# A first stage in a hand-written order: squares on two engines, sums on TensorE tile by tile, held-back loads and filler matmuls

## The chip, the cores and the metric

The kernel runs on one NeuronCore of a Trainium2 chip. The core has five engines that work side by side and meet only through semaphores: TensorE (PE in the profile, with its weight loads shown apart as PEld), VectorE (DVE), ScalarE (ACT), GpSimd (POOL) and SyncE (SP, which here only issues DMAs). [...] The metric is the device time of one launch in microseconds. Before the change three runs took 1020.61, 1021.97 and 1024.64 us, so the median is 1021.97 us.

## The reference

One inference step of a small diffusion backbone of two layers, on 128 context tokens and 256 latent tokens (384 columns in all), with 1024 features. Everything is fp32. What the first stage of the kernel computes is the start of layer 0:

```
def rmsnorm(x, g):
    xf = x.astype(jnp.float32)
    y = xf * lax.rsqrt(jnp.mean(xf * xf, axis=-1, keepdims=True) + EPS)
    return (y * g.astype(jnp.float32)).astype(x.dtype)

def adaln(cond, w_ada, b_ada):
    mod = jax.nn.silu(cond) @ w_ada + b_ada
    return jnp.split(mod[:, None, :], 6, axis=-1)

def modulate(h, shift, scale):
    return h * (1 + scale) + shift
...
    for l in range(DEPTH):
        sm, cm, gm, sf, cf, gf = adaln(c, w_ada[l], b_ada[l])
        h = modulate(rmsnorm(x, norm_mix_g[l]), sm, cm)
        j = l // N_MIXERS
        if l % N_MIXERS == 0:
            q, k, v = qkv_proj(h, w_qkv[j])
            o = neighbourhood_attention(q, k, v, cache_k[:, j], cache_v[:, j], rpb[j])
            mix = merge_heads(o) @ w_attn_out[j]
        else:
            mix = chunk_gmlp(h, w_gmlp_in[j], g_gmlp_v[j], w_spatial[j], b_spatial[j], w_gmlp_out[j])
        x = x + gm * mix
        h = modulate(rmsnorm(x, norm_ffn_g[l]), sf, cf)
        x = x + gf * conv_ffn(h, w_ffn_up[l], w_ffn_conv[l], b_ffn_conv[l], w_ffn_down[l])
```

The context tokens take the same path with a conditioning vector of their own and plain attention. The change is in the part from the load of `x` to the end of `h @ w_v`, the value projection of layer 0.

## The kernel before

The activations lie transposed: feature tile `x[k]` (k = 0 to 7) is 128 features on the partitions by 384 tokens. `GROUPS` splits the tokens into columns 0 to 127 (context) and 128 to 383 (latent), since the two have different modulation vectors.

A product that must keep fp32 accuracy is made of three matmuls (`mac`, L101): each operand is split into a rounded part `hi` and a rest `lo`, and hi*hi, hi*lo and lo*hi are summed in PSUM. For a weight tile, `load` (L88) issues a 512 KB DMA into a staging tile `st` (three buffers), ACT casts it to `hi` (L96), and DVE subtracts to get `lo` (L97). For the activations, `modulated` (L323) makes `u = x * scale * R` on DVE (L326), `hhi = u + shift` on ACT (L328) and `hlo` on DVE (L330), each once per token group.

The first stage runs as follows. SP issues the eight loads of `x` (L66), then the weights of the first modulation block `adw` (L127, two DMAs of 512 KB each), the tables `b_ada` (L132) and `prm` (L134), and then for each k one value-weight tile `st` and the next modulation block. ACT squares the tiles of `x`, DVE adds seven of them up in `sqacc` (L271), and six matmuls with a column of ones (`sums`, L282, for the total of seven and for the last tile) sum over the features. `rsqrt` (L306 to L316) turns the sums into `r` on DVE and POOL, and three matmuls with the identity (L300) spread `r` over all partitions as `R`, which ACT copies to SBUF (L409). A modulation block (`ada_block`, L136) is 16 small matmuls (L145) of the conditioning vectors with `adw`, a copy to SBUF on ACT (L149), a transpose on TensorE (L151) and three short DVE operations (L154, L157, L117) that write the shift and scale columns `mod` of one feature tile. Then for each k come the modulated tile, the value-weight tile, modulation block k + 1, and 18 matmuls (6 products of a 128-token block with a 512-column half) into six PSUM banks `acc` that stay open for all eight k. At the end ACT copies the six banks to `V`.

At the very start 18 matmuls of a tile of ones (`warm`, L80) run on TensorE while nothing else is there for it. fp32 matmuls show as two records each in the trace, a pass each.

The tile framework's scheduler sets the order of this stage on each engine, by priorities; only the matmuls that are marked `keep_in_program_order` are fixed. The attention loop behind it has its order written out by hand (`tc.manual_schedule`, L578): there each engine runs its instructions in the order of the program. In both cases an engine runs strictly in its order, so a waiting instruction holds up all behind it on that engine.

## Time and profile before

| what | value |
|---|---|
| runs before, median of three | 1021.97 us |
| profiled execution, its time | 1021.36 us |
| its span, first to last instruction | 1019.6 us |
| share of the chain that ended last: PE | 91% |
| first value matmul starts | 17.89 us |
| last value matmul is issued, and the next products start | 63.81 us |
| mean granted TensorE clock over the span | 0.993 |

All times in views of the trace count from the span's first instruction. The span leaves out 1.8 us of the profiled execution's own time. TensorE is busy nearly from end to end (98% of the span), so the stage's part of the total is when its last value matmul is done: what comes behind it follows on without a change of order.

### The profile page before, as it was taken

The numbers are of one execution on the slowest core, as the hardware profiler recorded it, in microseconds if no ns is written. First come the engines' busy times: TensorE is split into PE (matmuls) and PEld (weight loads), VectorE is DVE, ScalarE is ACT, GpSimd is POOL, SyncE is SP. The second block draws the span as 40 slices with busy tenths as digits, with TensorE's granted clock in tenths as the row PEclk, the third lists the DMA queues.
The fourth block names the chain that finished last, engine by engine and source line by source line (L and its number), as shares of the span: only waits on it lengthen the run. The fifth ranks groups of instructions, "written<-read, shape, count | busy, mean of one in ns | idle before, by whom it ended". The sixth has DMA issues, their size and how long they took to land.

```text
span 1019.6 us, 15979 instructions
## 1 busy us (share of the span) xinstructions
PE 998.2 (98%) x6030; PEld 948.6 (93%) x6030; DVE 775.7 (76%) x1588; ACT 480.6 (47%) x841; POOL 14.7 (1%) x29
## 2 busy tenths in 40 slices
PE   7999999999999999999999999999999999999996
PEld 6788888789999999999998889999999999999996
DVE  3546566577999888999979989888598777777652
ACT  3355556557655555433354434343485444443331
POOL 1000000000000000000000000000000000000000
PEclk8999999999999999999999999999999999999999
DMA  7874645633465545576737746566325434335521
GB/s 277 310 233 143 214 172 201 227 103 126 136 191 169 163 147 161 146 240 205 225 119 257 241 158 200 179 207 186 104 83 166 144 124 125 124 114 171 161 72 62
DMA packets 53932, 172.96 MB, mean 170 GB/s; under 512 B 6224, under 2 KB 12512, under 8 KB 53856
## 3 DMA queue, kind: packets, MB, share of 16 engines
q1 hardware_dynamic: 52992, 170.11, 51.9%
q0 software_dynamic: 432, 1.06, 0.3%
q8 instruction: 47, 0.77, 0.3%
q10 hardware_dynamic: 432, 0.79, 0.2%
q14 instruction: 29, 0.24, 0.1%
HBM read 169.31 MB, written 2.62 MB: 169 GB/s over the span
## 4 chain that ended last, share of the span: by engine, by line
PE 91%; DMA 3%; ACT 2%; DVE 1%; issue 1%; SPq 1%; POOL 0%; POOLq 0%; ACTq 0%
PE bank L103 28%; PE bank L105 28%; PE bank L104 28%; DMA kT<-in_ckT 2%; DMA adw<-in_w_ada 1%; PE bank L781 1%; PE bank L145 1%; PE bank L566 1%; PE bank L517 1%; PE bank L190 1%; PE bank L549 1%; PE bank L282 0%; ACT pr L534 0%; SPq L66 0%; PE bank L300 0%
## 5 line engine op out<-in xcount | busy, mean ns | idle before, releaser
L96 ACT CAST hi<-st 128x1024 fp32r<-128x1024 f32 (+1 forms) x192 | 197.7, 1031 | 302.3 <-PE bank L104 249.0
L105 PE MATMUL bank<-hhi,lo 128*128 128x384 f32 (+1 forms) x960 | 325.1, 339 | 0.2 <-DVE lo L109 0.2
L103 PE MATMUL bank<-hhi,hi 128*128 128x384 f32 (+1 forms) x960 | 325.0, 339 | 0.0
L104 PE MATMUL bank<-hlo,hi 128*128 128x384 f32 (+1 forms) x960 | 324.7, 338 | 0.0
L97 DVE TENSOR_TENSOR lo<-st,hi 128x1024 fp32r<-128x1024 f32 (+1 forms) x192 | 229.9, 1198 | 67.9 <-ACT hi L96 67.6
L105 PEld LDWEIGHTS bank<-hhi,lo 128*128 128x128 f32 x960 | 181.1, 189 | 0.5 <-DVE lo L109 0.5
L103 PEld LDWEIGHTS bank<-hhi,hi 128*128 128x128 f32 x960 | 181.1, 189 | 0.4 <-ACT kT L473 0.2
L104 PEld LDWEIGHTS bank<-hlo,hi 128*128 128x128 f32 x960 | 180.4, 188 | 0.1
L248 DVE CUSTOM_DVE_ANT_0 junk<-adw,cs 128x1024 bf16<-128x1024 f32 x112 | 136.5, 1219 | 1.0
L105 PE MATMUL bank<-ahi,lo 128*128 128x384 f32 x352 | 118.9, 338 | 0.0
L104 PE MATMUL bank<-alo,hi 128*128 128x384 f32 x352 | 118.9, 338 | 0.0
L103 PE MATMUL bank<-ahi,hi 128*128 128x384 f32 x352 | 118.7, 338 | 0.0
L104 PEld LDWEIGHTS bank<-alo,hi 128*128 128x128 f32 x352 | 66.1, 188 | 0.0
L105 PEld LDWEIGHTS bank<-ahi,lo 128*128 128x128 f32 x352 | 66.1, 188 | 0.0
L103 PEld LDWEIGHTS bank<-ahi,hi 128*128 128x128 f32 x352 | 66.1, 188 | 0.0
L103 PE MATMUL bank<-hi,hhi 128*128 128x512 f32 x144 | 57.6, 404 | 1.8 <-ACT hhi L328 1.8
L104 PE MATMUL bank<-lo,hhi 128*128 128x512 f32 x144 | 57.4, 398 | 0.0
L105 PE MATMUL bank<-hi,hlo 128*128 128x512 f32 x144 | 57.3, 399 | 0.0
L374 DVE SCALAR_TENSOR_TENSOR x<-bank,mod,x 128x128 f32<-128x128 f32 x64 | 23.8, 412 | 35.9 <-PE bank L105 35.9
L103 PE MATMUL bank<-mhi,hi 128*128 128x384 f32 x128 | 43.3, 339 | 0.0
L105 PE MATMUL bank<-mhi,lo 128*128 128x384 f32 x128 | 43.2, 338 | 0.0
L104 PE MATMUL bank<-mlo,hi 128*128 128x384 f32 x128 | 43.1, 337 | 0.0
(154 smaller groups left out, 1268.4 us busy)
## 6 DMA issues: line engine op xcount, KB each, us to landing
st<-in_w_up SPq DMA_DIRECT2D x88, 512.0 KB, 3.6
adw<-in_w_adaT SPq DMA_DIRECT2D x56, 512.0 KB, 3.7
adw<-in_w_ada SPq DMA_DIRECT2D x40, 512.0 KB, 5.8
st<-in_w_down SPq DMA_DIRECT2D x32, 512.0 KB, 3.6
st<-in_w_qk SPq DMA_DIRECT2D x16, 512.0 KB, 3.6
st<-in_w_gu SPq DMA_DIRECT2D x16, 512.0 KB, 4.3
st<-in_w_gv SPq DMA_DIRECT2D x16, 512.0 KB, 4.5
st<-in_w_gout SPq DMA_DIRECT2D x16, 512.0 KB, 4.4
```

Source lines behind the costliest of these rows:

```text
L96: nc.scalar.copy(hi[:, :n], st[:, :n])
L97: nc.vector.tensor_tensor(lo[:, :n], st[:, :n], hi[:, :n].bitcast(F32), ALU.subtract)
L103: nc.tensor.matmul(out, a[0], b[0], start=start, stop=False)
L104: nc.tensor.matmul(out, a[0], b[1], start=False, stop=False)
L105: nc.tensor.matmul(out, a[1], b[0], start=False, stop=stop)
L145: nc.tensor.matmul(pa[32 * j:32 * j + 32, 0:P], cond_s[:, 4 * hf + kk, :], w[hf][:, kk, P * q:P * q + P], start=(kk == 0), stop=(kk == 3), ...
L190: nc.tensor.matmul(self.pa[32 * j:32 * j + 32, 0:256], cond_s[:, k, :], t[:, 256 * j:256 * j + 256], start=(k == 0), stop=(k == KD - 1), t ...
L248: tc.keep_in_program_order(nc.vector.tensor_tensor_reduce(self.junk, t, self.cs[c], 1.0, 0.0, ALU.mult, ALU.add, m[:, c:c + 1]))
L374: nc.vector.scalar_tensor_tensor(x[m][:, a:b], ps[:, a:b], mod(l, gate, m, c), x[m][:, a:b], ALU.mult, ALU.add)
L517: nc.tensor.matmul(sc[hh][:, cols], q[qp][HS[hh], qs:qs + P], k[kp][HS[hh], ks], start=i == 0, stop=i == 2)
L549: nc.tensor.transpose((ta[:, o:o + P] if g < 2 else tb[:, o - 512:o - 512 + P]), pr[:, b, g * P:g * P + P], ident)
L566: nc.tensor.matmul(pv[64 * hh:64 * hh + 64, cols], vv[:, P * t + 64 * hh:P * t + 64 * hh + 64], pT[hh][:, o:o + n], start=start, stop=stop ...
```

## The change

The first stage, too, is put under `manual_schedule`, for PE, ACT, DVE and SP, and is written out anew:

- Loads of `x` alternate between the SP queue and the ACT queue; `b_ada` and `prm` go through POOL's queue, behind `cond`, and no longer through SP's.
- The 18 warm-up matmuls are replaced by `busy(n)`: n matmuls of a bf16 tile of ones, 128x512, into a bank that is not yet in use. They stand at ten places of TensorE's order, 26 in all: 8 at the start, 1 behind the sums of each of the tiles 0 to 5, 2 ahead of the first modulation block's matmuls, 2 ahead of its transpose, and 8 ahead of the first value matmul.
- ACT squares the even tiles, DVE the odd ones. There is no `sqacc`: TensorE sums every tile by itself (3 matmuls for each, 24 in all).
- The first two value-weight loads wait, through a small DVE memset into their staging tile (`v_load(True)`), until DVE is through with its squares and with `r`; the modulation blocks are loaded two ahead.
- For k = 0 the modulated tile reads `R` straight from PSUM; the copy of `R` to SBUF comes behind it on ACT, and the `lo` part of the first weight tile is made in two halves around `hlo`.
- For each k the order is: one product (3 matmuls), the 16 matmuls of modulation block k + 1, one product, the transpose of block k + 1, four products. The DVE order in a step is `mod`, `u`, `hlo`, `lo`.
- The last tile's products are split, three and three, with the copies to `V` shared between ACT and DVE and the first q/k weight tile made ready between them.

From the first q/k product on, the order on every engine is what it was.

```
+    written = tc.manual_schedule(engines={mybir.EngineType.PE, mybir.EngineType.Activation,
+                                          mybir.EngineType.DVE, mybir.EngineType.SP})
+    written.__enter__()
+    x = [cst.tile([P, NT], F32, name=f"x{k}") for k in range(KD)]
+    for k in range(KD):
+        (nc.sync, nc.scalar)[k % 2].dma_start(x[k], xT_in[:, k, :])
     cond = cst.tile([P, KD, 2], F32, name="cond")
     nc.gpsimd.dma_start(cond, cond_in)
-    x = [cst.tile([P, NT], F32, name=f"x{k}") for k in range(KD)]
-    for k in range(KD):
-        nc.sync.dma_start(x[k], xT_in[:, k, :])
+    b_ada = cst.tile([P, 2, 48], F32, name="b_ada")
+    nc.gpsimd.dma_start(b_ada, b_ada_in)
+    prm = cst.tile([P, NPRM], F32, name="prm")
+    nc.gpsimd.dma_start(prm, prm_in)
...
-    warm = bank(ps_ad)
-    for _ in range(18):
-        nc.tensor.matmul(warm[:, :P], ones, ones, start=True, stop=True)
...
+        def busy(n):
+            for _ in range(n):
+                nc.tensor.matmul(acc[4], fill[:, 0:P], fill, start=True, stop=True)
+
+        def v_load(late):
+            st = stg.tile([P, 1024], F32, name="st", tag="st")
+            if late:
+                nc.vector.memset(st[:, 0:1], 0.0)
+            return st
...
+        def shaped(k, R, between=None):
+            u = tmp.tile([P, NT], F32, name="t384", tag="t384", bufs=2)
+            for c, a, b in GROUPS:
+                nc.vector.scalar_tensor_tensor(u[:, a:b], x[k][:, a:b], mod(0, CM, k, c),
+                                               R[:, a:b], ALU.mult, ALU.mult)
+                nc.scalar.activation(hhi[:, k, a:b], u[:, a:b], AF.Identity, bias=mod(0, SM, k, c))
+            if between is not None:
+                between()
+            for c, a, b in GROUPS:
+                nc.vector.scalar_tensor_tensor(hlo[:, k, a:b], u[:, a:b], mod(0, SM, k, c),
+                                               hhi[:, k, a:b].bitcast(F32), ALU.add, ALU.subtract)
+
+        aw = {0: ada_load(0)}
+        busy(8)
+        ss = bank(ps_tb)
         for k in range(KD):
-            square(k, ("t384", "t384", "R0")[k % 3])
-        ss = sums(True)
-        ada_block(0, ps_ta)
-        Rp = rms(ss, True)
+            t = tmp.tile([P, NT], F32, name="t384", tag=("t384", "t384", "R0")[k % 3],
+                         bufs=1 if k % 3 == 2 else 2)
+            if k % 2:
+                nc.vector.tensor_tensor(t, x[k], x[k], ALU.mult)
+            else:
+                nc.scalar.activation(t, x[k], AF.Square)
+            if k == 4:
+                nc.scalar.activation(cond_s[:, :, 0:2], cond, AF.Silu)
+            for b in range(3):
+                nc.tensor.matmul(ss[:, 2 * b:2 * b + 2], t[:, b * P:(b + 1) * P], ones[:, 0:2],
+                                 start=(k == 0 and b == 0), stop=(k == KD - 1 and b == 2))
+            if k < 6:
+                busy(1)
+        st = [v_load(True)]
+        v_start(0, st[0])
+        aw[1] = ada_load(1)
+        r = inverse(ss)
+        st.append(v_load(True))
+        v_start(1, st[1])
+        busy(2)
+        sb = ada_products(aw.pop(0))
+        aw[2] = ada_load(2)
+        st.append(v_load(False))
+        v_start(2, st[2])
+        busy(2)
+        ada_turned(0, sb, ps_ta)
+        Rp = spread(r)
+        w = v_split(st.pop(0))
         R = tmp.tile([P, NT], F32, name="R0", tag="R0")
+        shaped(0, Rp, lambda: v_low(w, 0, 512))
         nc.scalar.copy(R, Rp[:, :NT])
-        acc = [bank(q) for q in (ps_mm, ps_mm, ps_mm, ps_sc, ps_sc, ps_ta)]
-        for k in range(KD):
-            modulated(0, SM, CM, k, R)
-            w = load(w_v[k])
-            if k < KD - 1:
-                ada_block(k + 1)
-            for half in range(2):
-                for b in range(3):
-                    mac(acc[3 * half + b], h(k, slice(b * P, (b + 1) * P)),
-                        wsel(w, half, slice(0, 512)), k == 0, k == KD - 1)
-        for b in range(3):
-            for half in range(2):
-                nc.scalar.copy(V[:, b, 512 * half:512 * half + 512], acc[3 * half + b])
-        nc.gpsimd.dma_start(sv_out, V[:, 0, :])
+        busy(8)
+        v_low(w, 512, 1024)
...
+        for k in range(KD - 1):
+            v_part(k, w, parts[:1])
+            sb = ada_products(aw.pop(k + 1))
+            if k + 3 < KD:
+                aw[k + 3] = ada_load(k + 3)
+                st.append(v_load(False))
+                v_start(k + 3, st[-1])
+            v_part(k, w, parts[1:2])
+            ada_turned(k + 1, sb, ps_tb)
+            w2 = v_split(st.pop(0))
+            shaped(k + 1, R)
+            v_low(w2, 0, 1024)
+            v_part(k, w, parts[2:])
+            w = w2
...
+        v_part(KD - 1, w, parts[:3])
+        v_out(0)
+        v_part(KD - 1, w, parts[3:])
+        ready()
+        v_out(1)
+        nc.gpsimd.dma_start(sv_out, V[:, 0, :])
         p = products()
-        ready()
```

`v_split` is the ACT cast of a staged tile to `hi`, `v_low` the DVE subtraction for `lo`, `v_part` the `mac` calls of the given products, `v_out` the copies to `V`; `ada_products` and `ada_turned` are the two halves of the old `ada_block`, and `spread` is the old tail of `rms`.

Three places show what moved. The first is the start of TensorE's order, up to the spread of `r` (`t` are squared tiles, `bank` any PSUM bank). Before:

```order
L80 MATMUL bank<-ones 128x128 x18
L282 MATMUL bank<-ones,sqacc 128x2 x3
L282 MATMUL bank<-ones,t_213 128x2 x3
L145 MATMUL bank<-adw,cond_s 32x128 x16
L151 MATMUL bank<-ident,ada_sb 128x128
L300 MATMUL bank<-ident,rr 128x128 x3
```

Now, from the sums of tile 5 on, without the rows that only repeat a filler:

```order
L458 MATMUL bank<-ones,t_223 128x2 x3
L410 LDWEIGHTS fill
L410 MATMUL bank<-fill 128x512
L458 MATMUL bank<-ones,t_229 128x2 x3
L458 MATMUL bank<-ones,t_234 128x2 x3
L145 MATMUL bank<-adw,cond_s 32x128 x16
L154 MATMUL bank<-ident,ada_sb 128x128
L304 MATMUL bank<-ident,rr 128x128 x3
```

Two groups of sums have become eight, one for each tile, with fillers between them; the block's matmuls, the transpose and the spread still follow in the old order.

The second place is one step of the k loop on DVE (`t` is `u` here; `rr` above is `r`). Before, for tile 2:

```order
L154 TENSOR_TENSOR mod_143<-bank,b_ada 128x2x2
L157 TENSOR_TENSOR mod_143<-mod_143,bank 128x2x2
L117 SCALAR_TENSOR_TENSOR mod_143<-mod_143,prm 128x2
L326 SCALAR_TENSOR_TENSOR t_385<-x_95,mod_143,R_259 128x128
L326 SCALAR_TENSOR_TENSOR t_385<-x_95,mod_143,R_259 128x256
L97 TENSOR_TENSOR lo<-st,hi 128x1024
L330 SCALAR_TENSOR_TENSOR hlo<-t_385,mod_143,hhi 128x128
L330 SCALAR_TENSOR_TENSOR hlo<-t_385,mod_143,hhi 128x256
```

Now:

```order
L157 TENSOR_TENSOR mod_131<-bank,b_ada 128x2x2
L160 TENSOR_TENSOR mod_131<-mod_131,bank 128x2x2
L124 SCALAR_TENSOR_TENSOR mod_131<-mod_131,prm 128x2
L436 SCALAR_TENSOR_TENSOR t_416<-x_95,mod_131,R_299 128x128
L436 SCALAR_TENSOR_TENSOR t_416<-x_95,mod_131,R_299 128x256
L442 SCALAR_TENSOR_TENSOR hlo<-t_416,mod_131,hhi 128x128
L442 SCALAR_TENSOR_TENSOR hlo<-t_416,mod_131,hhi 128x256
L430 TENSOR_TENSOR lo<-st,hi 128x1024
```

The 1024-wide subtraction that makes `lo` has moved from ahead of `hlo` to behind it, to the end of the step.

The third place is TensorE in the same loop. Before, where a step meets the next modulation block:

```order
L145 MATMUL bank<-adw,cond_s 32x128 x16
L103 MATMUL bank<-hi,hhi 128x512
L104 MATMUL bank<-lo,hhi 128x512
L151 MATMUL bank<-ident,ada_sb 128x128
L105 MATMUL bank<-hi,hlo 128x512
```

Now the same, with the three matmuls of the step's first product ahead of the block:

```order
L110 MATMUL bank<-hi,hhi 128x512
L111 MATMUL bank<-lo,hhi 128x512
L112 MATMUL bank<-hi,hlo 128x512
L145 MATMUL bank<-adw,cond_s 32x128 x16
L154 MATMUL bank<-ident,ada_sb 128x128
```

In the second piece one product (three matmuls, rows that read like the first three) stands between the block and the transpose, and 12 matmuls follow the transpose before the next step's first three. The step's second matmul already reads `lo`, and only the third reads `hlo`; before, the block's 16 matmuls often came between the transpose and the first use of the new tile.

## The prediction

> **What bounds the kernel now.** I read the page first, then the chain of waits in the first 30 us, the stage cut into stretches, and the timeline of one step.

> ```profile
> PE 91%; DMA 3%; ACT 2%; DVE 1%; issue 1%; SPq 1%; POOL 0%; POOLq 0%; ACTq 0%
> ```

> TensorE carries the end. A microsecond counts only if it moves the moment at which TensorE is done with the value products, which is where its first 384-column product starts:

> ```profile
> 63.81 0.34 PE L103 MATMUL bank<-hhi,hi 128*128 128x384 f32 x1
> ```

> The chain of waits shows how the stage begins (start, length, what):

> ```profile
> 4.97 7.21 DMA adw<-in_w_ada
> 12.22 1.95 PE bank L145 x28
> ...
> 14.60 0.44 PE bank L151
> 15.05 1.05 PE bank L300 x6
> 16.12 0.48 ACT R L409
> 16.60 0.94 ACT hi L96
> ...
> 17.89 0.73 PE bank L103 x2
> ```

> The first modulation block waits for its weights until 12.22; its matmuls, the transpose, the spread of `r`, a copy and a cast follow one by one, and value products start at 17.89. In stretches (length, then busy us of PE, PEld, DVE, ACT, POOL, granted clock, DMA share, GB/s):

> ```profile
> 5.43:8.84 3.41, 2.15 (x19) 1.95 (x18) 2.23 (x4) 2.98 (x7) 0.00 (x0) 1.00 1.06 317
> 8.84:12.25 3.41, 1.87 (x20) 1.58 (x20) 1.28 (x3) 0.52 (x1) 0.18 (x1) 1.00 1.01 399
> 12.25:15.67 3.42, 2.96 (x33) 2.43 (x34) 1.04 (x6) 0.27 (x1) 1.39 (x4) 0.50 1.03 419
> 15.67:19.08 3.41, 1.60 (x11) 0.84 (x10) 2.25 (x5) 2.12 (x4) 0.00 (x0) 1.00 1.01 399
> 19.08:22.49 3.41, 3.41 (x31) 2.37 (x33) 0.38 (x1) 0.00 (x0) 0.00 (x0) 0.50 0.33 127
> 22.49:63.81 41.32, 41.32 (x346) 30.62 (x339) 23.96 (x58) 19.36 (x35) 0.30 (x1) 1.00 0.77 268
> ```

> The clock is granted in steps of 3.41 us; a stretch with PE busy for 1.87 or 1.60 is followed by one at half clock, one with 2.15 or 2.96 is not. The two half-clock stretches cost up to 1.7 us each. From 22.49 TensorE never pauses. So of the 63.81 us only the part before about 22 has slack to win.

> **The change, part by part.** Starts, weight loads and sums first:

> ```profile
> 0.74 3.71 SPq L66 DMA_DIRECT2D x<-in_xT  x8
> ...
> 0.73 1.28 ACT L69 ACT_TABLE_LOAD   x1 [0.73 <-PEq L891]
> ...
> 1.36 6.21 PE L80 MATMUL bank<-ones 128*128 128x128 f32 x36 [1.36 <-DVE mhalf L82]
> ...
> 5.74 3.65 ACT L269 ACTIVATE t<-x 128x384 f32<-128x384 f32 x7
> ...
> 10.21 0.83 PE L282 MATMUL bank<-ones,sqacc 128*128 128x2 f32 x6 [2.64 <-DVE sqacc L271]
> 10.90 0.81 PE L282 MATMUL bank<-ones,t 128*128 128x2 f32 x6
> ...
> 11.75 0.16 DVE L309 TENSOR_SCALAR rv<-bank 128x3 f32<-128x3 f32 x1 [1.59 <-PE bank L282]
> ...
> 13.45 0.16 DVE L316 SCALAR_TENSOR_TENSOR rr<-rt,ry 128x3 f32<-128x3 f32 x1
> ...
> DMA to landing us min/median/max: 2.5/4.4/4.8
> ...
> 19.79 0.63 PE L104 MATMUL bank<-lo,hhi 128*128 128x512 f32 x1
> 20.21 0.63 PE L105 MATMUL bank<-hi,hlo 128*128 128x512 f32 x1
> ```

> (The landing line is that of `x`.) ACT now issues four loads ahead of its table load: 4 x 0.46 (3.71 by 8) = 1.9 us. Its first square ends at 0.7 + 1.9 + 1.3 + 0.2 + 0.5 = 4.6, which the eight first fillers cover: at half clock 0.42 each (20.21 less 19.79) they last from 1.4 to 4.8. Splitting `x` over two queues I cost at nothing: the DMA engines' share is already 1.0.

> TensorE's sums grow from 12 passes to 48. One group of six starts every 10.90 - 10.21 = 0.69 us at full clock, so eight take 5.5 us; six fillers between them add 1.4 (no bf16 filler is in the trace; the nearest row is a 512-column product at 0.24, below; bounds 0, hidden under weight loads, and 0.42). From 4.8 that ends at 11.7, with 0.3 for half clock until 5.43 at **12.0**. Data would allow 10.1 (the last `x` lands by 4.0 + 4.8 = 8.8, a square 0.56, a group 0.69), so TensorE has become the bound of the sums. They ended at 11.71. Taking DVE's six additions off the path buys nothing by this. `r` follows by the same DVE and POOL operations 1.9 us later (11.71 to 13.61), at 13.9.

> The block's weights: `b_ada` and `prm` (252 KB) now go ahead of them, through POOL's queue.

> ```profile
> cond<-in_cond POOLq DMA_DIRECT2D x1, 8.0 KB, 4.3
> ```

> At 399 GB/s the tables take 0.6 us, so `adw` lands at 12.8. Lower bound 12.2 (nothing is delayed); upper bound 14.2, if each of two further small POOL loads holds up the engines as `cond` may do (4.3 us for 8 KB, where 192 KB of `x` took 2.5). I take 12.8, since the bytes are few. The first held-back value load waits for a memset behind DVE's last square (about 9.4), and on SP's queue block 1 waits behind it; both still go out before `adw` has landed, and follow it at 1.25 us for 512 KB (at 419 GB/s): 14.1 for the value tile, whose cast starts at 14.2 at the earliest, and 16.6 for block 1, wanted at 17.8. The second waits for `r` at 13.9, with block 2 behind it, which TensorE holds until 13.8 anyway; it lands near 17.8 and is wanted at 19.6. I cost these waits at nothing; with `adw` late they would be late with it. The block then runs at full clock, 1.0 instead of 1.95, to 13.8; copy and transpose to 14.4; spread (six passes, 0.7) to 15.2, `r` being ready. The modulated tile reads `R` in PSUM, so copy (0.48) and cast (0.94) leave the path. Instead eight fillers of 0.23 stand ahead of the first product, to 17.0; DVE and ACT make `hhi` by 16.1, behind that cover, and the half `lo` and `hlo` by 17.0. Value products start at **17.0, 0.9 earlier**.

> Now the step. Times of PE, ACT and DVE in one step of before:

> ```profile
> 48.69 1.08 PE L145 MATMUL bank<-adw,cond_s 128*32 128x128 f32 x32
> ...
> 49.70 0.50 PE L103 MATMUL bank<-hi,hhi 128*128 128x512 f32 x1
> ...
> 50.51 0.28 PE L151 MATMUL bank<-ident,ada_sb 128*128 128x128 f32 x1
> ...
> 50.54 0.48 PE L103 MATMUL bank<-hi,hhi 128*128 128x512 f32 x1
> ...
> 50.82 0.16 DVE L154 TENSOR_TENSOR mod<-bank,b_ada 128x4 f32<-128x4 f32 x1 [0.74 <-PE bank L151]
> ...
> 51.41 0.75 DVE L326 SCALAR_TENSOR_TENSOR t<-x,mod,R 128x128 f32<-128x128 f32 x2
> ...
> 51.80 0.91 ACT L328 ACTIVATE hhi<-t,mod 128x128 fp32r<-128x128 f32 x2 [1.61 <-DVE t L326]
> ...
> 52.74 0.48 DVE L330 SCALAR_TENSOR_TENSOR hlo<-t,mod,hhi 128x256 fp32r<-128x256 f32 x1
> ...
> 53.42 0.39 PE L103 MATMUL bank<-hi,hhi 128*128 128x512 f32 x1
> ...
> 53.68 1.23 DVE L97 TENSOR_TENSOR lo<-st,hi 128x1024 fp32r<-128x1024 f32 x1 [0.46 <-ACT hi L96]
> ...
> 54.22 0.97 PE L145 MATMUL bank<-adw,cond_s 128*32 128x128 f32 x28
> ```

> A step takes 54.22 - 48.69 = 5.53. Call the transpose T (50.51). DVE is through with `mod`, `u` and `hlo` at T + 2.7 (52.74 + 0.48); `lo`, now last, ends at T + 3.9. TensorE has 12 matmuls behind the transpose: they are done at T + 2.9 (53.42, so 0.24 each), the next tile's first matmul needs only `hhi`, and its second, at T + 3.15, needs `lo`. It **waits 0.75 us**, and the rest of TensorE's queue with it: the next block, its copy, its transpose. From `lo` to the next transpose are two matmuls (0.5), the block (1.0 from 48.69 to 49.70, some 0.1 to get to it) and a product (0.8 to 50.51): 2.4. A step is 3.9 + 2.4 = 6.3, a loop through both engines. Bounds: no wait at all, if DVE's chain is 0.75 shorter; 0.46 more, if the cast of `hi` is late, as at 53.68. I take 0.75, since every length in it is a row of the same operations.

> Sum: 17.0, to the first transpose in the loop 2.6 (a product 0.7, the block 1.1, a product 0.8), six steps of 6.3 = 37.8, and from the last transpose 3.9 and 17 matmuls of 0.24, 7.9: **65.3 against 63.81, 1.5 later**. The first steps gain 1.7 to 2.6 from the clock and the start, and seven waits of 0.75 (5.3) take them back.

> Behind the stage, the third q/k weight load now waits for the last `lo` (57.4 + 3.9 = 61.3), and the loads of `kT` behind it on SP's queue with it:

> ```profile
> 45.69 9.57 SPq L448 DMA_DIRECT2D st<-in_w_qk  x3
> ...
> 68.81 0.62 ACT L108 CAST khi<-kT 128x512 fp32r<-128x512 f32 x1
> ```

> It was at 54.9 (the third of the three). `kT` goes out near 62, takes some 4, and is wanted at 70.3: hidden by 4 us. Were that gone, each us late would count once.

> The profiled execution took 1021.36: plus 1.5, 1022.9. Its time lies 0.6 below the median of three, so the median would be **1023.5**.

> [...]

> **Rivals.**

> *No wait in the step.* If `lo` is in time, steps stay 5.5 and the seven waits go: 65.3 - 5.3 = 60.0, 3.8 earlier than before, 1018.2 for the median. For it: PE at 100% from 22.49 on, DVE 58% busy. Against it: the chain above, whose order is given. With a start at 16, if the last eight fillers cost less, it reaches 1017.2.

> *Half clock during the sums.* Mechanism: the gate counts matmul streaming, not weight loads; a sums group streams two columns a pass and loads weights for the rest, so from 8.84 on the stretch counts as idle. It decides somewhere between 1.87 and 2.15 busy of 3.41. Price: 3.2 us of sums are left at 8.84; doubled, they end at 15.2; `r` at 17.1; two fillers, the block, its copy and transpose and the spread at half clock reach 19.9, eight fillers of 0.42 reach 23.3: the start is 6.3 later than summed, 1029.8. If the clock is back at 15.67, the start is 20.2: 1026.7. For it: 1.87 with twelve such passes led to half clock. Against it: six 512-column fillers stand among the sums, and PE has no gaps there.

> *POOL's queue holds up the block's weights* (the gain is not there): `adw` at 14.2, the start 1.4 later, 1024.9.

> **Chances.** The wait in the step as summed 0.56 (its own range 1021.5 to 1025.5), no wait 0.24, half clock 0.12, late weights 0.08. 0.5% is 5.1 us, about what a measurement can tell from no change here: below 1016.9 or above 1027.1. Faster: 0.13, half of the second case, where the start is early too. Slower: 0.11, most of the third and a tail of the first. Same: 0.76. The range, 1016.5 to 1027, leaves out 0.2.

> **What would show it.** The second matmul of each step with idle time ahead of it released by `lo` (about 0.75), steps of 6.3; sums ending near 12.0 with TensorE filled; granted clock 1.0 from 5.4 on; first value product near 17, next products near 65. No wait ahead of the second matmul, or a half-clock stretch behind 8.84, would make it wrong.

## The result and the profile after

Eight runs of the changed kernel have a median of 1030.38 us (1025.97 to 1032.87), eight of the kernel before one of 1021.34 (1019.45 to 1024.64). The ratio is 1.0082, with a 95% interval of 1.0067 to 1.0098: the change costs 9.0 us in the medians. The forecast was 1023.5, its range ended at 1027.0. The profiled execution of the changed kernel took 1027.10 us, with a span of 1025.3 and a mean granted clock of 0.992: 5.74 more than that of the kernel before.

The page's chain by engine, for the changed kernel. TensorE still carries the end, and DVE's share has grown from 1% to 3%:

```profile
PE 93%; DVE 3%; ACT 2%; DMA 1%; issue 1%; POOL 0%; SPq 0%; POOLq 0%; ACTq 0%; DVEq 0%
```

The timeline of the changed kernel (start, length, engine, line, operation, count): the issue of the first block's weights on SP's queue, TensorE from the sums to the first value product, and the first of the next products:

```profile
4.59 0.80 SPq L134 DMA_DIRECT2D adw<-in_w_ada  x2
...
8.39 1.03 PE L458 MATMUL bank<-ones,t 128*128 128x2 f32 x6
9.67 1.28 PE L458 MATMUL bank<-ones,t 128*128 128x2 f32 x6
11.19 2.56 PE L458 MATMUL bank<-ones,t 128*128 128x2 f32 x12
...
14.55 1.94 PE L145 MATMUL bank<-adw,cond_s 128*32 128x128 f32 x32
...
18.74 1.96 PE L410 MATMUL bank<-fill 128*128 128x512 bf16 x8
20.35 0.58 PE L110 MATMUL bank<-hi,hhi 128*128 128x512 f32 x1
...
69.39 0.33 PE L110 MATMUL bank<-hhi,hi 128*128 128x384 f32 x1
```

The sums end at 11.19 + 2.56 = 13.75 instead of 11.71, the first value product starts at 20.35 instead of 17.89, and the next products at 69.39 instead of 63.81. From there to the end of the span it is 955.9 us (955.8 before). In this pair of profiles the whole loss, 5.58 of 5.74, stands ahead of the next products, in two pieces: 2.46 in front of the value products and 3.12 within them (49.04 instead of 45.92).

The first piece, in stretches of the changed kernel (length, then busy us of PE, PEld, DVE, ACT, POOL, granted clock, DMA share, GB/s):

```profile
5.22:8.64 3.42, 3.42 (x31) 3.31 (x32) 1.12 (x2) 1.26 (x4) 0.00 (x0) 1.00 1.05 376
8.64:12.05 3.41, 3.41 (x18) 3.23 (x18) 0.57 (x2) 0.41 (x1) 0.00 (x0) 0.50 0.58 205
12.05:15.46 3.41, 3.41 (x30) 2.51 (x34) 0.56 (x3) 0.00 (x0) 1.33 (x3) 0.50 1.01 404
15.46:18.88 3.42, 3.42 (x30) 2.42 (x23) 0.65 (x5) 1.21 (x2) 0.24 (x1) 0.50 0.57 180
18.88:22.29 3.41, 3.41 (x44) 1.98 (x42) 2.60 (x6) 1.26 (x3) 0.00 (x0) 1.00 0.92 344
```

Between 5.22 and 8.64 PE is shown busy for every one of the 3.42 us, and the clock halves all the same, for three stretches in a row. The busy column cannot tell why. The chain of waits splits the same time into its pieces (start, length, what):

```profile
5.92 0.24 PE bank L410
6.16 0.56 PE bank L458 x6
6.72 0.24 PE bank L410
6.96 0.56 PE bank L458 x6
...
9.88 1.07 PE bank L458 x6
```

A group of six sum passes takes 0.56 at full clock and streams 6 x 2 columns in it, while PEld, the weight loads, is busy for 3.31 of the 3.42 us. Only the fillers, 0.24 each, stream many columns. In the stretch ahead of the half clock stand four of them, about 1 us of 3.42. At half clock a group takes 1.07.

The second piece is the wait in the step. TensorE's waits of the changed kernel in the first 70 us (total, times, longest), and one step in its timeline:

```profile
PE bank L111 <- DVE lo L430: 4.3, 7, 0.7
```

```profile
42.36 0.27 PE L154 MATMUL bank<-ident,ada_sb 128*128 128x128 f32 x1
...
44.58 0.48 DVE L442 SCALAR_TENSOR_TENSOR hlo<-t,mod,hhi 128x256 fp32r<-128x256 f32 x1 [0.15 <-ACT hhi L438]
...
44.98 1.22 DVE L430 TENSOR_TENSOR lo<-st,hi 128x1024 fp32r<-128x1024 f32 x1
45.26 0.40 PE L110 MATMUL bank<-hi,hhi 128*128 128x512 f32 x1
46.25 0.50 PE L111 MATMUL bank<-lo,hhi 128*128 128x512 f32 x1 [0.60 <-DVE lo L430]
...
46.92 1.08 PE L145 MATMUL bank<-adw,cond_s 128*32 128x128 f32 x32
...
48.73 0.27 PE L154 MATMUL bank<-ident,ada_sb 128*128 128x128 f32 x1
```

The first matmul of a new tile starts at 45.26 and the second, which needs `lo`, at 46.25 instead of 0.24 later: 0.75 is lost, though the view of waits counts 0.60, because it lets the first matmul end late. The step from transpose to transpose is 48.73 - 42.36 = 6.37.

The first block's weights were not late. Their two loads, in the view of DMA issues of the changed kernel and of the kernel before (KB each, median us from issue to landing):

```profile
adw<-in_w_ada SPq DMA_DIRECT2D x2, 512.0 KB, 5.6
```

```profile
adw<-in_w_ada SPq DMA_DIRECT2D x2, 512.0 KB, 6.8
```

With the tables on POOL's queue and half of `x` on ACT's, they land sooner after their issue than before, and TensorE never waits for them.

### The profile page after: what moved, and what is told of

It reads as the page before. It is cut to its first block, busy times and chain, and to the rows that moved or that the text cites. A ratio compares the mean times of both kernels' runs of the same rounds, so it can differ in the third digit from the quotient of the medians.

```text
span 1025.3 us, 16031 instructions
## 1 busy us (share of the span) xinstructions
PE 1002.9 (98%) x6056; PEld 949.6 (93%) x6056; DVE 777.0 (76%) x1592; ACT 478.6 (47%) x835; POOL 15.7 (2%) x31
## 4 chain that ended last, share of the span: by engine, by line
PE 93%; DVE 3%; ACT 2%; DMA 1%; issue 1%; POOL 0%; SPq 0%; POOLq 0%; ACTq 0%; DVEq 0%
PE bank L111 28%; PE bank L112 28%; PE bank L110 28%; PE bank L651 1%; PE bank L868 1%; PE bank L602 1%; PE bank L634 1%; PE bank L193 1%; PE bank L410 1%; PE bank L145 1%; DVE lo L430 1%; DMA adw<-in_w_ada 1%; PE bank L458 1%; DMA kT<-in_ckT 1%; ACT hhi L438 1%
## 5 line engine op out<-in xcount | busy, mean ns | idle before, releaser
L103 ACT CAST hi<-st 128x1024 fp32r<-128x1024 f32 (+1 forms) x184 | 189.4, 1030 | 303.7 <-PE bank L111 248.0
L104 DVE TENSOR_TENSOR lo<-st,hi 128x1024 fp32r<-128x1024 f32 (+1 forms) x184 | 220.2, 1198 | 67.3 <-ACT hi L103 66.9
```

The source lines that it names most:

```text
L103: nc.scalar.copy(hi[:, :n], st[:, :n])
L104: nc.vector.tensor_tensor(lo[:, :n], st[:, :n], hi[:, :n].bitcast(F32), ALU.subtract)
```

## The experiments

All kernels below start from the changed kernel ("after"), unless it says otherwise. This table is from their traces and times; "ready" is the end of the last operation on `r`, "rest" is the span less the start of the next products. Times and ratios are medians against runs of the kernel before on the same chip.

| kernel | `r` ready | first value product | next products | rest | profiled time | median of runs | ratio to before |
|---|---|---|---|---|---|---|---|
| before | 13.61 | 17.89 | 63.81 | 955.8 | 1021.36 | 1021.34 | 1 |
| after | 15.64 | 20.35 | 69.39 | 955.9 | 1027.10 | 1030.38 | 1.0082 [1.0067, 1.0098] |
| again | 18.45 | 22.49 | 71.53 | 955.1 | 1028.43 | one run | |
| wide | 14.70 | 17.41 | 66.45 | 958.7 | 1027.02 | 1025.44 | 1.0045 [1.0024, 1.0065] |
| lo | 15.47 | 19.86 | 62.67 | 958.4 | 1022.92 | 1022.09 | 1.0015 [0.9998, 1.0033] |
| both | 13.93 | 16.64 | 59.48 | 956.3 | 1017.57 | 1017.52 | 0.9970 [0.9956, 0.9984] |
| nofill | 12.50 | 15.03 | 57.84 | 957.5 | 1017.21 | 1017.96 | 0.9973 [0.9962, 0.9984] |
| few | 12.91 | 15.04 | 58.10 | 958.1 | 1018.01 | 1017.90 | 0.9970 [0.9957, 0.9983] |
| add7 | 13.23 | 15.76 | 58.57 | 957.5 | 1017.94 | 1017.85 | 0.9967 [0.9948, 0.9986] |
| queues | 13.61 | 16.61 | 60.43 | 958.1 | 1020.34 | 1018.56 | 0.9978 [0.9964, 0.9991] |
| late | 13.32 | 15.86 | 58.70 | 954.8 | 1015.37 | 1013.12 | 0.9916 [0.9900, 0.9933] |
| before_late | 14.29 | 18.30 | 65.31 | 952.2 | 1019.28 | 1020.56 | 0.9987 [0.9975, 1.0000] |
| after_late | 15.36 | 19.95 | 69.00 | 952.6 | 1023.38 | 1024.67 | 1.0043 [1.0027, 1.0060] |

**again**: the changed kernel unchanged, executed and profiled once more.

> The changed kernel as it is, profiled a second time. Theory: two things make it slower, one on each side of the first value product: TensorE at half clock from 8.64 to 18.88 us (first value product at 20.35), and a wait of 0.6 to 0.7 us for lo ahead of the second matmul of each step (steps of 6.4 us where they were 5.5). Both show again; next products start near 69.4. Rival: the first profile caught an odd execution; then the clock or the start differ by more than 1 us, or a third loss stands behind the stage, since the median of eight lay 3.3 us above the profiled one.

TensorE's timeline, sums only, and one stretch of the same execution:

```profile
4.88 1.28 PE L458 MATMUL bank<-ones,t 128*128 128x2 f32 x6
...
14.00 2.56 PE L458 MATMUL bank<-ones,t 128*128 128x2 f32 x12 [0.24 <-issue]
```

```profile
10.04:13.45 3.41, 3.41 (x18) 3.23 (x18) 0.57 (x2) 0.52 (x1) 0.00 (x0) 1.00 0.02 8
```

In this execution every group is shown with 1.28, as the groups at half clock are in the first profile: the clock was at half from the first group to the last. The clock column says 1.00 there, but this trace has no clock entry ahead of 20.28, and the view counts time without an entry as full clock; the durations decide. So the mean clock of this execution, 0.997, is too high. The first value product came at 22.49, 2.1 later than in the first profile: the rival that the start differs by more than 1 us came true, while no third loss shows behind the stage (rest 955.1). Same program, same order; what differs, counted in steps of 3.41 us, is where its matmuls fall. In the first profile the eight fillers (1.49 to 4.88) nearly fill the stretch that ends at 5.22, and the clock comes up there. Counted back from 20.28 in steps of 3.41, a stretch here ends at 3.21 and the next at 6.63: by this count the fillers are split between two, and the clock does not come up.

**wide**: the sums multiply by all 128 columns of ones, not by two. The number of passes, their weights and the order stay the same; only the streamed columns grow, and one column in 128 of the sums' bank (in PSUM; the rows of these matmuls have it as `bank<-ones,t`) is read.

```
-                nc.tensor.matmul(ss[:, 2 * b:2 * b + 2], t[:, b * P:(b + 1) * P], ones[:, 0:2],
+                nc.tensor.matmul(ss[:, P * b:P * b + P], t[:, b * P:(b + 1) * P], ones,
...
-        r = inverse(ss)
+        rv = tmp.tile([P, 4], F32, name="rv", tag="rv", bufs=2)
+        r = rsqrt(ss[:, 0:NT].rearrange("p (b c) -> p b c", c=P)[:, :, 0], rv[:, 0:3], 1.0 / D)
```

> One edit: the matmuls of the sums stream all 128 columns of the tile of ones where they streamed 2. Passes, weight loads and order are the same, and a pass of 128 columns started every 0.11 us at full clock in the warm-up of the kernel before, like a pass of 2 columns, so TensorE's time at full clock does not change. Theory (the clock gate counts streaming, and 2-column passes count as idle): granted clock 1.0 from 5.2 on, sums done at 11.2 instead of 13.8, first value product at 15.8 instead of 20.35, 4.5 us off the total: 0.4% above the kernel before. Rival (the gate closes for another reason: the first fillers, the constant data of ones, or any TensorE work that waits): half clock again behind 8.6, first value product at 20.4, total unchanged.

The stretches of this kernel's sums:

```profile
7.33:10.74 3.41, 3.41 (x29) 3.26 (x29) 0.75 (x2) 1.15 (x3) 0.00 (x0) 1.00 0.80 319
10.74:14.16 3.42, 3.37 (x52) 2.85 (x51) 0.54 (x4) 0.00 (x0) 0.88 (x1) 1.00 0.57 174
14.16:17.57 3.41, 3.36 (x25) 1.88 (x18) 2.39 (x11) 2.30 (x5) 0.00 (x0) 1.00 1.00 393
```

PE is as busy as in the changed kernel, 3.41 of 3.41, but the clock stays at 1.0, and the first value product comes at 17.41 instead of 20.35 or 22.49. It was expected at 15.8: in this execution the clock came up only at 7.33 (12 matmuls in the 2.45 us ahead of it, 29 in the 3.41 behind), and the wider groups take a little longer (0.83 in the timeline of "both", 0.72 in that of the changed kernel, each at full clock). In every profile with 2-column sums in 48 passes (after, again, lo, after_late) the sums ran at half clock in part or in whole; in every one with 128 columns (wide, both and the five kernels built on it) the clock, once up, stayed up through them: granted 1.00 in wide from 7.33 on, groups of 0.83 in "both" behind a first one of 1.26, and `r` ready at 13.93 at the latest in "both" and the five, where 2 columns had it at 15.36 at the earliest. So at the same busy time, 3.42 and 3.41 us in a stretch, the next one had a clock of 0.50 behind passes of 2 columns and of 1.00 behind passes of 128: what made the difference is the streamed columns, not the time in which PE has an instruction.

**lo**: DVE makes `lo` ahead of `hlo` in each step.

```
-            shaped(k + 1, R)
-            v_low(w2, 0, 1024)
+            shaped(k + 1, R, lambda: v_low(w2, 0, 1024))
```

> One edit: in each step DVE makes lo ahead of hlo, in the order of the kernel before; all else is the changed kernel. Theory (lo at the end of DVE's step holds TensorE up): lo ends 2.9 us behind the transpose instead of 3.9, before TensorE's second matmul of the next tile (3.15); the seven waits go, steps of 5.5 to 5.6, next products near 64, 5.3 us off the total: 0.3% above the kernel before. Rival: hlo, now last on DVE, takes the wait over at the third matmul; it ends at 3.25 for the first 128 columns, wanted at 3.4; if it is late the step stays above 6 and the total falls by less than 2 us.

One step in this kernel's timeline:

```profile
39.13 0.27 PE L154 MATMUL bank<-ident,ada_sb 128*128 128x128 f32 x1
...
40.69 1.22 DVE L430 TENSOR_TENSOR lo<-st,hi 128x1024 fp32r<-128x1024 f32 x1
...
41.82 0.74 DVE L442 SCALAR_TENSOR_TENSOR hlo<-t,mod,hhi 128x128 fp32r<-128x128 f32 x2
42.02 0.40 PE L110 MATMUL bank<-hi,hhi 128*128 128x512 f32 x1
42.26 0.40 PE L111 MATMUL bank<-lo,hhi 128*128 128x512 f32 x1
...
44.62 0.27 PE L154 MATMUL bank<-ident,ada_sb 128*128 128x128 f32 x1
```

`lo` now ends 2.78 behind the transpose (41.91 less 39.13) and not 3.84 (46.20 less 42.36), the second matmul follows the first by 0.24, and the step is 5.49. From the first value product to the next products it is 42.81 instead of 49.04: 6.2 less, 0.88 for each of seven steps: the lost 0.75 and a slower matmul behind it (0.34 to the next one, where `lo` has 0.23). The half clock behind the sums is still there.

**both**: the two edits together.

> Both edits together. Theory: the two losses are on two sides of the first value product and add up: first value product at 15.8, steps of 5.5, next products near 59.3, 9.8 us off the changed kernel: 4 us or 0.4% below the kernel before. Rival: the gain of one is taken back by a transfer that is then late (modulation weights two blocks ahead need 1.5 MB in each 5.5 us); then steps vary and the total falls by less than 7 us.

Its timeline:

```profile
16.64 0.58 PE L110 MATMUL bank<-hi,hhi 128*128 128x512 f32 x1
...
59.48 0.34 PE L110 MATMUL bank<-hhi,hi 128*128 128x384 f32 x1
```

By the ratios, wide takes 0.37 points off the changed kernel's 0.82 and lo 0.67; together they take 1.12, about the sum. So the two pieces are separate, and with both repaired the stage as written by hand beats the kernel before, by 0.3%.

**nofill**: "both" without the six fillers among the sums.

```
-            if k < 6:
-                busy(1)
```

> The kernel with both edits, without the six fillers among the sums. Its groups of six passes start every 0.88 us where a filler stands between them and take 0.79 where none does (2.38 for three). Theory (the gate counts streamed columns, and a filler is nearly hidden under weight loads): the clock stays at 1.0, sums and r come about 0.5 us earlier (r at 13.4 against 13.93), next products near 59.0, 1017.0. The prediction's own price of a filler (0.24 each) would make it 1.4 earlier: r at 12.5. Rival (the fillers are what keeps the clock up): a half-clock stretch behind the sums, the first value product 2 to 5 us later than 16.64, 1020 to 1023.

The sums in its timeline, in one piece:

```profile
4.88 5.80 PE L458 MATMUL bank<-ones,t 128*128 128x128 f32 x48
```

With 128 columns the clock stayed up without fillers among the sums: 0.12 a pass (5.80 by 48), where a pass at half clock took 0.21 in again (1.28 by 6). Against the expectation, they had not been hidden under weight loads: without them the sums end 1.4 earlier, the first value product comes 1.6 earlier. That is the prediction's price, 0.24 each. The next products start at 57.84, 1.64 earlier, and yet the median is no better (1017.96 against 1017.52). In the two traces 1.3 of the 1.6 are given back behind the stage (rest 957.5 and 956.3).

**few**: as nofill, and three instead of eight fillers ahead of the first value product.

```
-        busy(8)
+        busy(3)
         v_low(w, 512, 1024)
```

> As the run without fillers among the sums, and with three of the eight fillers ahead of the first value product. Theory: the eight stood beside DVE and ACT making hhi and the first half of lo (ready 0.05 to 0.4 us before they ended), so at most 0.4 us more is won: next products near 58.7, 1016.7, against the kernel before -0.3 to -0.5%. By the prediction, which let the fillers set the start from 15.2 to 17.0, five fewer are worth 1.15 us: 57.9, 1015.9.

Its timeline:

```profile
15.04 0.50 PE L110 MATMUL bank<-hi,hhi 128*128 128x512 f32 x1 [0.30 <-ACT hhi L438]
```

Now TensorE waits for `hhi`. From `r` ready to the first value product it takes 2.13 instead of 2.53 in nofill: the eight fillers cost 0.4, not 1.15, since `hhi` and `lo` are made beside them. In this execution `r` was ready 0.4 later, for no reason in the edit, so the first value product stands where it stood in nofill, and the median is the same too (1017.90 and 1017.96).

**add7**: "both" with the squares as before the change (all on ACT, seven added up on DVE, two groups of sums), and 20 fillers ahead of the sums.

```
+            square(k, ("t384", "t384", "R0")[k % 3])
...
+        busy(20)
+        for i, t in enumerate((sq["acc"], sq["last"])):
...
```

> The kernel with both edits, but with the squares as in the kernel before: all on ACT, seven added up on DVE, two groups of sums (12 passes in place of 48), with 20 fillers in one piece ahead of them so that TensorE streams while it waits. Theory (48 passes made TensorE the bound of the sums): squares follow the landings of x to 9.4, the last addition ends near 9.6, two groups end at 11.2, r at 13.1: 0.8 us earlier than 13.93, next products near 58.7, 1016.7. Rival (additions on DVE are what the change took off the path): r at 14.4 or later, next products 60 or later, 1018 or more.

Its timeline:

```profile
9.91 0.83 PE L455 MATMUL bank<-ones,sqacc 128*128 128x128 f32 x6
10.58 0.83 PE L455 MATMUL bank<-ones,t 128*128 128x128 f32 x6
```

The sums end at 11.42 and `r` is ready at 13.23, as expected: 0.7 earlier than with 48 passes and fillers between them, 0.7 later than nofill. So taking DVE's additions off the path is worth something only if TensorE's 48 passes are not slowed by fillers, or by the clock.

**queues**: "both" with all loads of `x` and the tables on SP's queue, in the order of before.

```
-        (nc.sync, nc.scalar)[k % 2].dma_start(x[k], xT_in[:, k, :])
+        nc.sync.dma_start(x[k], xT_in[:, k, :])
...
+        nc.sync.dma_start(b_ada, b_ada_in)
+        nc.sync.dma_start(prm, prm_in)
```

> The kernel with both edits, but with all loads of x on SP's queue and the two tables on it too, behind the first block's weights, as in the kernel before. Theory (the split of the loads costs and brings nothing, since the sums set the start): the first block's weights land near 12.2 in place of 11.0, the block still waits for TensorE's own queue at 12.5, first value product at 16.6 within 0.3, 1017.5 within 1. Rival (the other queues are what makes the start early): weights or x later by 1.2 us or more, first value product at 17.8 or later, 1018.7 or more.

Its timeline:

```profile
18.61 1.07 PE L143 MATMUL bank<-adw,cond_s 128*32 128x128 f32 x28 [0.47 <-DMA adw<-in_w_ada]
```

The first value product is where it was, but the second block's weights, behind on the same queue, are now late for the second block, and the next products start 0.95 later. So `x` and the tables on several queues are worth about 1 us in this pair of traces, at the second block and not at the first; which of the two does it was not tried. The medians (1018.56 and 1017.52, with their ratios) do not tell the two apart.

**late, before_late, after_late**: the question was where nofill's gain went. TensorE's waits between 150 and 225 us, for before, after and nofill (total, times, longest):

```profile
PE bank L190 <- DMA adw<-in_w_ada: 2.0, 3, 0.8
```

```profile
PE bank L193 <- DMA adw<-in_w_ada: 3.8, 3, 1.9
```

```profile
PE bank L193 <- DMA adw<-in_w_ada: 3.8, 3, 2.1
```

And for "both":

```profile
PE bank L193 <- DMA adw<-in_w_ada: 3.7, 3, 2.0
```

Near the end of the attention loop, some 120 us behind the next products, TensorE waits three times for weights of modulation blocks. They cost 1.8 more in the changed kernel than in the one before; in the kernels built on it they are 3.7 to 3.8 too, but 3.2 in queues and 2.3 in add7. So the waits themselves did not take nofill's gain: they are the same in "both", which does not have it. What differs is the clock. In nofill two stretches at half clock follow, in "both" only one:

```profile
179.50:182.95 3.45, 2.30 (x14) 1.49 (x15) 1.78 (x5) 1.16 (x4) 0.00 (x0) 0.50 0.92 361
182.95:186.37 3.42, 3.42 (x13) 3.42 (x12) 2.14 (x4) 2.16 (x5) 0.00 (x0) 0.50 0.71 286
```

```profile
183.27:186.70 3.43, 2.93 (x17) 2.13 (x18) 1.45 (x7) 1.79 (x6) 0.00 (x0) 0.50 1.00 362
186.70:190.00 3.30, 3.30 (x20) 3.01 (x20) 1.93 (x3) 1.52 (x3) 0.00 (x0) 1.00 0.58 225
```

Later nofill has a third, from 210.25, behind a wait for DVE of 1.86 that "both" has too (1.9), by its mean clock (0.997 against 0.993) without half clock behind it:

```profile
209.01 0.42 PE L110 MATMUL bank<-ohi,hi 128*128 128x384 f32 x1 [1.86 <-DVE x L376]
...
210.67 0.52 PE L112 MATMUL bank<-ohi,lo 128*128 128x384 f32 x1
```

The edit, made in nofill ("late"), in the kernel before and in the changed kernel, moves these three blocks behind the first output tile's six products:

```
-            if last:
-                ada.run(3)
-            else:
+            if not last:
...
         output(0, range(6), ps_mm)
+        ada.run(3)
```

> The kernel with both edits and without fillers among the sums; in addition the last three modulation blocks of the attention loop are moved on TensorE behind the first six products of the first output tile, which need no new load. In the run without this, TensorE waits there for their weights three times, 1.07 + 0.71 + 2.07 = 3.85 us at 119 to 123 us behind the next products, and 6.83 us at half clock follow, though the stage itself had become 1.6 us faster than with the fillers and the total had not. Theory (these waits and the half clock behind them took back what the stage won, and their phase spreads the times): the waits go, 3.9 us less, and up to 3.4 us of half clock; next products to end 950.5 to 954 in place of 957.5, 1011 to 1014. Rival (the blocks only wait elsewhere, or the exponentials they covered come to light): 1017 to 1018.

> The kernel before with only that same move of three modulation blocks in the attention loop. It tells how much of the gain there has nothing to do with the change. Its waits there are 0.77 + 0.64 + 0.63 = 2.04 us. Theory: 2.0 us less and perhaps 1.7 of half clock, next products to end 952 to 954 in place of 955.8, 1017 to 1019, so that the kernel above stays 5 to 7 us ahead of it (its stage ends at 57.84 against 63.81). Rival (nothing is won by it): 1020.8.

> The changed kernel with only that same move of three modulation blocks. Its waits there were 1.22 + 0.63 + 1.94 = 3.79 us. Theory: 3.8 us less and 1.7 to 3.4 of half clock: 1023 to 1026 against 1030.4, and still 6 to 8 above the kernel before with the same move, since the stage ends 5.6 to 7.7 later. Its profile is also one more look at the sums: a half-clock stretch must begin within 3.4 us of their sixth group, and the first value product stand at 19.9 to 22.5. Rival (nothing is won by the move): 1030.

TensorE's waits of "late" in the same place:

```profile
PE bank L632 <- ACT pT L639: 2.2, 1, 2.2
```

The waits for weights are gone and one for ACT has taken their place, 2.2 instead of 3.8. The move changes the order only between the last score matmul (`khi` with `qlo`) ahead of the three blocks and the first matmul of `values(6)` behind them. With the traces cut at the starts of these two (us):

| kernel | next products to last score matmul | on to `values(6)` | on to the end |
|---|---|---|---|
| both | 118.93 | 11.34 | 825.98 |
| nofill | 117.35 | 12.71 | 827.46 |
| late | 119.17 | 9.57 | 826.08 |
| before | 120.23 | 8.30 | 827.24 |
| before_late | 118.31 | 8.03 | 825.84 |
| after | 118.58 | 11.43 | 825.88 |
| after_late | 117.08 | 9.58 | 825.89 |

Between "both" and nofill the two losses, 1.4 and 1.5, stand where nofill has its extra half clock. The move itself is worth the change in the middle column: 3.1 in nofill, 1.9 in the changed kernel and 0.3 in the kernel before, where 2.0 of waits for weights gave way to 2.2 for ACT. The last column falls by 1.4 in the two that have a half-clock stretch near 210 us without the move (nofill from 210.25, the kernel before from 213.60). The first column differs by up to 1.9 either way, though nothing in it was changed. The medians moved by 4.8 (nofill), 5.7 (changed kernel) and, against the expectation, only 0.4 (kernel before). So the kernel before gains nothing to speak of by the move; why the changed kernel's median falls by more than its trace shows is open, as a profile exists for one run only of each kernel. "late" has the best time of all: 1013.12, a ratio of 0.9916 to the kernel before.

With the three blocks moved in both, the changed kernel stands 4.1 above the kernel before in the medians (1024.67 and 1020.56), against 3.7 in the start of the next products (69.00 and 65.31). Expected were 6 to 8. Without the move it stands 9.0 above it. So about half of the loss in the medians goes with the order at these three blocks, and half belongs to the stage.

## Why the prediction was wrong

The step that failed is "granted clock 1.0 from 5.4 on", and with it the sums at 12.0 and the start at 17.0. In its place the trace shows half clock from 8.64 to 18.88, sums until 13.75 and the start at 20.35. The forecast took the case "wait in the step as summed" and priced half clock during the sums as a rival of its own, at 0.12. Both happened together. Of the 4.1 us between 65.3 and 69.39, 3.35 are the start and 0.74 the time from there on (49.04 for 48.3). The median lies another 2.7 higher than forecast: it was put 0.6 above the profiled run and is 3.3 above it.

- *The rule read from the profile.* The text took busy time for what decides, somewhere between 1.87 and 2.15 of 3.41 us, from stretches of before with 1.87 and 1.60 (half clock followed) and 2.15 and 2.96 (it did not). But 0.83 + 0.81 of the 1.87 were twelve sum passes of two columns. Without them that stretch had 0.2 to 0.4 us of streaming. That much is not what it takes either: at a wait for DVE near 210 us among 384-column matmuls (1.86 in before and nofill, 1.85 in after) a stretch with 1.58 us busy (after, 217.08 to 220.50) kept the clock, while 1.55 (before, 210.19 to 213.60, and nofill, 206.84 to 210.25) lost it. The busy column was taken for activity, and it does not follow the streamed columns: a pass of 2 columns shows 0.09 us in it (0.56 by 6), one of 128 at most 0.12 (5.80 by 48). "PE has no gaps there", the argument against the rival, was true and beside the point. The rival (its "gate" is what sets the granted clock) named the right mechanism by wide, with 1.00 where the changed kernel has 0.50, and "six fillers stand among the sums" was not put into numbers: four of 0.24 in 3.42 us are 28%.
- *Its price.* The rival put the start at 20.2 if the clock came back at 15.67 and at 23.3 if not; it came back at 18.88 in one profile, with the start at 20.35, and the other execution had it at 22.49. Its upper time, 1029.8, is near the median, by luck: in neither trace is the start as late as 23.3, and 3.3 us of the median stand in no trace.
- *The sums.* "One group of six starts every 0.69" was too long: at full clock it is 0.56, while a filler is 0.24 as taken. With 5.08 for the start and 0.3 for the first group at half clock, 8 x 0.56 + 6 x 0.24 gives 11.3, not 12.0. Half clock made it 13.75, 2.4 more; from there to the first value product it took 6.6 instead of the 4.5 of "both" (12.12 to 16.64), 2.1 more. That TensorE bounds the sums was right, and also that taking DVE's additions off the path buys little: with the additions back, add7 was between "both" and nofill.
- *The start at 17.0.* Near what a clock that holds gives with the wide sums, 17.41 and 16.64, but in part by luck. For the sums as they were written, 11.3 and the 4.5 give an estimate of 15.8 at full clock; the 0.69 a group, too long for them, is close to the 0.67 that a wide group takes in "both". "Eight fillers ... to 17.0" were on the path by 0.4 only.
- *Late weights.* Wrong: "`adw` lands at 12.8" was near 11.0 (the issue at 4.59, 0.80 for the two, 5.6 to landing). The tables on POOL's queue held nothing up. The split of `x`, costed at nothing, and the tables off SP's queue together bring 1 us in "both", where all on SP's queue makes the second block late.
- *The step.* Right in place, cause and size: 0.75 lost at the second matmul, released by `lo`, seven times, and steps of 6.37 for 6.3. With it removed, 42.8 for the value products, where the prediction's 60.0 - 17.0 gives 43.0. The rival without a wait, 1018.2, is close to what "both" measured, 1017.52.
- *Behind the stage.* "Hidden by 4 us" was right for the loads it named: the waits in the first 20 us of the next products are 0.6 and 0.2, before and after alike. But the text took the rest to be the same by the order of instructions. The order is the same and the time is not: 952 to 959 us in thirteen profiles. At the end of the attention loop the modulation weights come 2.0 us late in the kernel before and 2.3 to 3.8 in those built on the change that keep the blocks in place, and 3.41 us at half clock follow in the changed kernel and in "both", 6.83 in nofill; a later wait for DVE, of 1.85 or 1.86 us, brings another 3.41 in before and nofill and none in the changed kernel. In the profiled pair this cancelled out (955.8 and 955.9); in the medians it did not.

What stays open: the median of the changed kernel lies 3.3 above its own profiled run, while that of before equals its own. A start that varies by 2.1 (20.35 and 22.49) and a rest that varies by several us could give such a spread, but no profile of one of the longer runs exists. More half clock on record does not explain the three longest (1031.56, 1032.70 and 1032.87): their mean granted clock is 0.993, that of the profiled run 0.992. Half clock ahead of a trace's first clock entry, as in again, does not show in that mean.

## What to carry to other kernels

Read TensorE's activity in streamed columns: here matmuls that load 128 columns of weights to stream two were shown busy for 3.42 of 3.42 us, and the clock fell to 0.50 behind them; widening them kept it at 1.00 (wide), for at most 0.03 us more a pass (0.16 by 6), and needed no fillers between (nofill). In a loop in which two engines take turns, let the other engine make first what the next matmul needs first; two swapped lines cost 0.9 us in a step of 5.5. And look at the waits behind a stage before counting its gain: of 1.6 us won in the stage the trace gave 1.3 back, in half clock behind waits 120 and 150 us later that were as long without the gain.
